# Expert products of a PEER layer: three load buffers per weight, splits one step ahead of their own kind, first product by halves of the tokens

## The chip, the cores and the metric

One core of a Trainium2 chip runs the whole layer in one launch. The metric is the device time of that launch in microseconds (us). The kernel before takes 3207.91 us, the median of three runs (3204.24 to 3208.45). A difference of 0.2% (6.4 us) is about what a measurement of this kernel can tell from no change.

## The reference

The layer is a state-space and convolution mixer, and then a retrieval layer of 16384 one-neuron experts. Only the last part matters here:

```
q = (hf @ wq).reshape(t, 8, 2, 128); s = einsum("thpd,hpkd->thpk", q, sub_keys)
sv, si = top_k(s, 16)                       # 16 of 128 keys on either side
best, flat = top_k(sums of pairs, 16)       # 16 experts of each of 8 heads
experts = i1 * 128 + i2;  gates = softmax(best)
act = gelu(einsum("pd,ped->pe", xb, u_tab[eb]), approximate=False)
out = einsum("pe,ped->pd", gb * act, v_tab[eb])     # 128 experts of each token
```

There are 1024 tokens of 1024 channels, in eight blocks of 128. A gated residual and a final RMSNorm follow. All numbers are float32.

## The kernel before, in words

The kernel is written in one order by hand: each engine executes its instructions in the order in which the program issues them, and a buffer that is still in use makes the engine that wants it wait. Loads of weights are issued on SP's queue, which is also in order: a load whose buffer is not free holds up all loads behind it.

The last stage, the **experts' stage**, is a little over half of the time. Five blocks of tokens (640 tokens, `ND = 5`) take the dense way: the products with *all* experts are formed, 128 experts at a time, and experts that a token did not choose have the gate 0. The other three blocks take the sparse way: they gather the rows of their own experts from DRAM.

*Dense, on TensorE (PE).* A step `In(e)` is the first product of 128 experts: `multiply_u` (L980) multiplies the weights `u`, split in a high and a low part `uh`, `ul` of float32r, with the tokens `hh2`, `hl2`, in 48 matmuls of 320 tokens. Two PSUM tiles `pa` of 320 tokens each take the sums; the pool has three. Then ScalarE (ACT) applies Gelu (`ga`, L1380, one instruction for each half), VectorE (DVE) multiplies with the gates `gm` (L1384), ACT and DVE split the result in `wh` (L1386) and `wl` (L1390). A step `Out` is half of the columns of the second product of 128 experts: 15 matmuls of 512 columns with the weights `v`, split in `vh`, `vl`. Eight `Out` steps sum in PSUM, then DVE adds the sums to the output (L1434). The order of steps is `In` 0 to 7, then again and again 8 `Out`, 1 `In`, 8 `Out`, 7 `In`: 128 `In` and 256 `Out` in all. The first products of e = 0 to 2 are started ahead of the loop.

*Splits.* `hi_lo` (L59, L60): ACT copies to the high part, and the low part is a subtraction, on GpSimd (POOL) for `u`, on DVE for `v`. There are two buffers each of `uh`, `ul`, `vh`, `vl`, and also of the loaded `u`, `v` and `gm`.

*Sparse.* `gathered` (L1266) asks POOL for one row of an expert per token (128 rows of 4 KB, 512 KB, L1275) into one of five buffers `gr`; DVE then forms a dot product (L1297) or adds a multiple (L1309). There are 768 such rows of work. `advance` (L1341) puts them between the steps of the products by fixed shares: 18 units for an `In`, 11 for an `Out`. `choosing` does the choice of experts of the last block beside the first groups. `finish` (L1246) does residual and norm of a sparse block, and borrows two `gr` buffers for it.

What orders the loads and splits is the loop at L1478: at step n the load of step n + 2 is issued, then the split of step n + 1, then the rest of the Gelu step before, then the products:

```
        for x in seq[:2]:
            x.load()
        for n, x in enumerate(seq):
            if n + 2 < len(seq):
                seq[n + 2].load()
            if n + 1 < len(seq):
                seq[n + 1].split()
            ...
            x.mm()
```

Of the kernel before, what the change touches and what calls it, by code (L numbers as in the profile page):

```python
# [8 lines left out]
F32 = mybir.dt.float32  # L9
# [28 lines left out]
ND = 5                   # token blocks whose experts go through dense products; the others gather theirs  # L38
TD = ND * P
TH = TD // 2  # L40
NS = 7                   # token blocks whose experts are chosen before the products
NGB = 5                  # rows of gathered experts on chip
IN_US, OUT_US = 18, 11    # shares of the gather steps beside 128 experts' first product and half of their second
GE = 8                   # blocks of 128 experts between two sums into the output

# The pairs of ranks (i, j) that can be among the top ones: (i + 1)(j + 1) <= 16; those of the upper half have
# (i + 1)(j + 1) <= 8. Pieces are (i0, i1, j0, j1); sums stand in lexicographic order, numbers of experts with the first 20 ahead.
# [15 lines left out]
def mm3(nc, out, a, b, n, start=True, stop=True):  # L63
    """out += sum_k a[k].T @ b[k] in float32 accuracy; a, b give (hi, lo) pairs of a k."""
# [7 lines left out]
def layer_kernel(ctx, tc, A, dbg=None):  # L72
# [8 lines left out]
    # ------------------------------------------------------------------ constants  # L81
# [9 lines left out]
    def rsqrt(dst, src, scale, n):  # L91
        """dst = 1 / sqrt(src * scale + eps) on a small tile, with one Newton step."""
# [15 lines left out]
    row_dram = dram.tile([1, D], F32, name="row_dram")          # gate of the second sublayer  # L108
# [3 lines left out]
    g_dram = dram.tile([ND, 2, P, P, P // 2], F32, name="g_dram")   # gates: [token block, half, second key, first key, token]  # L112
# [32 lines left out]
    # chunks of w_in_t: 0-3 z, 4-7 x, 8-9 B, 10-11 C, 12-15 GLU value, 16-19 GLU gate, 20 dt  # L145
# [14 lines left out]
    def modulate(j):  # L160
        """h1 of the tokens or of the context in [channel, token] layout, split."""
# [9 lines left out]
    # ------------------------------------------------------------------ modulation, norm 1  # L171
    with ExitStack() as st:
# [22 lines left out]
        # sums of squares of the tokens from the transposed tensors  # L195
# [17 lines left out]
        # rows of scale and shift for both conditions, then as columns  # L213
# [52 lines left out]
    # ------------------------------------------------------------------ work beside the matrix products  # L266
    queue, later, spare, call = [], [], [0.0], [0]

    def beside(us):
        """Emits queued instructions that hold VectorE for about this long; a step below zero rests until the next call."""  # L270
# [16 lines left out]
    def ask():  # L287
        """Loads the next two column blocks for modulation()."""
        while asked[0] < 24 and len(ready) < 2:
            j = asked[0]  # L290
            ready[j] = lpr.tile([P, KD, P], F32, name="ld")
            nc.sync.dma_start(ready[j], ada[:, :, 2048 + j * P:2048 + (j + 1) * P])
            asked[0] += 1

    def modulation():
        """The gate of the first sublayer as a row on all partitions, shift and scale of the second as columns."""
# [40 lines left out]
    def key_products():  # L337
        """M = wq @ subkeys.T of every head and side, a half of one at a time."""
# [26 lines left out]
    # ------------------------------------------------------------------ input projection  # L365
    with ExitStack() as st:
# [51 lines left out]
        def layer_norm():  # L418
            """Channel LayerNorm and swish of the convolution group."""
# [26 lines left out]
        def time_steps(pdt):  # L446
            """softplus(v) = max(v, 0) + log1p(e), e = exp(-|v|); log1p by its series where e is small."""
# [25 lines left out]
            # decay to the end of a chunk (times dt), and over a chunk  # L473
# [80 lines left out]
    # ------------------------------------------------------------------ state-space scan, both directions  # L554
# [1012 lines left out]
```

## Time and profile before

| | |
|---|---|
| median of 3 runs | 3207.91 us |
| span of the profiled execution | 3212.8 us |
| PE, DVE, POOL, ACT busy, whole span | 90%, 84%, 62%, 31% |
| experts' stage, from its first product to its last | 1202.3 to 3195.2 us |
| PE, DVE, POOL, ACT busy in that stage | 1864, 1676, 1431, 506 us of 1993 |
| DMA engines busy in that stage | 85%, 296 GB/s |

The profiled execution's own time is not given apart from its span; the span is 0.15% above the median of the runs. A matmul's record is longer than its share of the pipe, so neighbours overlap and PE counts as busy even where it is not at its peak: the distance between starts tells its pace. Waits are put down to the event that came last.

### The profile page before, as it was taken

To read this page: it belongs to the slowest core of one execution; us is meant where nothing else is said; L and a number is where in the kernel's file an instruction comes from. 1 tells how busy PE (TensorE), PEld (TensorE's weight loads), DVE (VectorE), ACT (ScalarE), POOL (GpSimd) and SP (SyncE) were. 2 spreads that over 40 slices of the span, in tenths; PEclk is the share of its full clock that TensorE was granted. 3 is DMA by queue.
4 is the path that set the end of the run, shared out by engine and by line. 5 is a ranking of instruction groups with operands and counts; after the bars stand their busy time and mean duration, and the time that the engine had idled before them with its cause. 6 is when DMAs were issued, how large, how long until landed. Compare 5 with 4: busy or idle time off the path is not lost.

```text
span 3212.8 us, 41810 instructions
## 1 busy us (share of the span) xinstructions
PE 2880.9 (90%) x14905; PEld 2383.1 (74%) x14905; DVE 2693.3 (84%) x4828; ACT 1002.9 (31%) x1584; POOL 2002.0 (62%) x1478
## 2 busy tenths in 40 slices
PE   7999777998888768988999999999999899999996
PEld 4777676754555558877788788888888788888884
DVE  5897888559999997889898887888898888888896
ACT  3224323324555552322222222222222222222222
POOL 0222455316666777777677676776687677777773
PEclk8999998999999879999999999999999999999998
DMA  6111454341212237877888888899889889889883
GB/s 203 59 40 40 127 160 147 99 164 60 85 80 105 105 125 264 314 262 268 298 276 306 303 303 309 315 313 323 302 310 325 303 299 331 308 303 319 303 312 109
DMA packets 334113, 721.09 MB, mean 224 GB/s; under 512 B 24512, under 2 KB 167120, under 8 KB 332624
## 3 DMA queue, kind: packets, MB, share of 16 engines
q0 software_dynamic: 110592, 402.70, 35.5%
q1 hardware_dynamic: 223312, 315.72, 28.6%
q8 instruction: 117, 1.92, 0.2%
q14 instruction: 92, 0.75, 0.1%
HBM read 656.99 MB, written 61.35 MB: 224 GB/s over the span
## 4 chain that ended last, share of the span: by engine, by line
DVE 31%; DMA 19%; PE 18%; issue 16%; POOL 12%; ACT 2%; SPq 0%; POOLq 0%; DVEq 0%; ACTq 0%
POOL gr L1275 7%; DMA gr<-in_peer_v_dram,idx 6%; DMA v<-in_peer_v_dram 5%; DMA gr<-in_peer_u_dram,idx 5%; PE pa L985 4%; PE pa L67 4%; DVE gr L1297 3%; DVE o L1206 2%; POOL ul L60 2%; DVE ob L1198 2%; DVE cfm L407 2%; DVE oh L1076 2%; PE pv L1416 2%; PE pq L946 2%; PE pv L1417 2%
## 5 line engine op out<-in xcount | busy, mean ns | idle before, releaser
L1275 POOL DMA_INDIRECT gr<-in_peer_u_dram,idx x384 | 521.3, 1358 | 216.2 <-DVE gr L1297 130.5
L1275 POOL DMA_INDIRECT gr<-in_peer_v_dram,idx x384 | 504.6, 1314 | 212.4 <-DVE h2T L1309 124.2
L1309 DVE SCALAR_TENSOR_TENSOR h2T<-gr,wv,h2T 128x1024 f32<-128x1024 f32 x381 | 535.5, 1405 | 61.5 <-DMA gr<-in_peer_v_dram,idx 55.1
L1297 DVE SCALAR_TENSOR_TENSOR gr<-gr,h2T 128x1024 f32<-128x1024 f32 x384 | 514.3, 1367 | 73.2 <-DMA gr<-in_peer_u_dram,idx 62.2
L1416 PE MATMUL pv<-vl,wh 128*128 128x512 f32 x1280 | 523.6, 409 | 56.2 <-DVE vl L60 53.9
L1415 PE MATMUL pv<-vh,wl 128*128 128x512 f32 x1280 | 515.5, 403 | 15.2 <-ACT vh L59 15.0
L1417 PE MATMUL pv<-vh,wh 128*128 128x512 f32 x1280 | 512.5, 400 | 0.0
L985 PE MATMUL pa<-hl,uh 128*128 128x320 f32 x2000 | 329.7, 315 | 52.6 <-ACT ga L1380 48.6
L60 POOL TENSOR_TENSOR ul<-u,uh 128x1024 fp32r<-128x1024 f32 x128 | 332.9, 2601 | 66.7 <-ACT uh L59 58.1
L59 ACT ACTIVATE vh<-v 128x512 fp32r<-128x512 f32 x256 | 161.1, 630 | 643.1 <-DMA v<-in_peer_v_dram 522.0
L1416 PEld LDWEIGHTS pv<-vl,wh 128*128 128x128 f32 x1280 | 244.8, 191 | 148.4 <-DVE vl L60 91.9
L985 PEld LDWEIGHTS pa<-hl,uh 128*128 128x128 f32 x2000 | 305.2, 191 | 65.2 <-ACT ga L1380 58.2
L985 PE MATMUL pa<-hh,ul 128*128 128x320 f32 x2000 | 322.2, 315 | 4.5 <-POOL ul L60 4.5
L60 DVE TENSOR_TENSOR vl<-v,vh 128x512 fp32r<-128x512 f32 x256 | 186.4, 728 | 157.0 <-ACT vh L59 152.0
L985 PE MATMUL pa<-hh,uh 128*128 128x320 f32 x2000 | 313.6, 309 | 0.0
L985 PEld LDWEIGHTS pa<-hh,ul 128*128 128x128 f32 x2000 | 307.3, 193 | 5.3 <-POOL ul L60 5.3
L1415 PEld LDWEIGHTS pv<-vh,wl 128*128 128x128 f32 x1280 | 244.7, 191 | 84.0 <-ACT vh L59 26.2
L985 PEld LDWEIGHTS pa<-hh,uh 128*128 128x128 f32 x2000 | 298.4, 188 | 0.0
L1417 PEld LDWEIGHTS pv<-vh,wh 128*128 128x128 f32 x1280 | 244.7, 191 | 54.5
L1200 POOL TENSOR_TENSOR o<-ob,tr 128x512 f32<-128x512 bf16 x160 | 216.1, 1352 | 108.9 <-DVE ob L1198 99.7
L1184 PEld LDWEIGHTS pg<-o,o 128*128 128x128 f32 x1280 | 173.5, 207 | 131.1 <-issue 62.3
L1386 ACT ACTIVATE wh<-ga 128x640 fp32r<-128x640 f32 x128 | 94.8, 740 | 543.5 <-DVE ga L1384 527.3
(351 smaller groups left out, 4661.9 us busy)
## 6 DMA issues: line engine op xcount, KB each, us to landing
u<-in_peer_ut_dram SPq DMA_DIRECT2D x128, 512.0 KB
v<-in_peer_v_dram SPq DMA_DIRECT2D x256, 256.0 KB
g_dram<-stg SPq DMA_DIRECT2D x10, 4096.0 KB
gm<-g_dram SPq DMA_DIRECT2D x64, 640.0 KB
ld<-in_ada_w_dram SPq DMA_DIRECT2D x24, 512.0 KB
w<-in_w_in_t_dram SPq DMA_DIRECT2D x21, 512.0 KB
raw<-in_ada_w_dram SPq DMA_DIRECT2D x8, 1024.0 KB
h2T<-in_wqT_dram SPq DMA_DIRECT2D x16, 512.0 KB
```

The lines of the kernel that those rows point to most:

```text
L59: nc.scalar.activation(hi, src, AF.Copy)
L60: (eng or nc.vector).tensor_tensor(lo, src, hi.bitcast(F32), op=OP.subtract)
L67: nc.tensor.matmul(out, a(k)[i], b(k)[j], start=start and t == 0 and k == 0, stop=stop and t == 2 and k == n - 1)
L985: nc.tensor.matmul(pa[half], x[:, k], y[:, k, half * TH:half * TH + TH], start=t == 0 and k == 0, stop=t == 2 and k == KD - 1)
L1184: nc.tensor.matmul(pg[:, j], o2[:, j], o1[:, j], start=True, stop=True)
L1200: nc.gpsimd.tensor_tensor(o2.rearrange("p t j -> p j t"), ob, tr[:, 1, None, ts].to_broadcast([P, P, 4]), op=OP.mult)
L1275: nc.gpsimd.indirect_dma_start(out=g, out_offset=None, in_=A[t], in_offset=bass.IndirectOffsetOnAxis(ap=idx[:, b, e:e + 1], axis=0))
L1297: nc.vector.scalar_tensor_tensor(g, g, 1.0, h2, op0=OP.mult, op1=OP.mult, accum_out=act[:, e:e + 1])
L1309: nc.vector.scalar_tensor_tensor(ac, g, wv[:, e:e + 1], ac, op0=OP.mult, op1=OP.add)
L1415: nc.tensor.matmul(Out.pv[t], wl[:, sl], self.vh, start=i == 0, stop=False)
L1416: nc.tensor.matmul(Out.pv[t], wh[:, sl], self.vl, start=False, stop=False)
L1417: nc.tensor.matmul(Out.pv[t], wh[:, sl], self.vh, start=False, stop=i == GE - 1)
```

## The change

1. `v` gets three buffers (`NV = 3`). `u` keeps the two of its pool, and every third `u` goes to `spare`, a part of the old token tile `h2T` that held the weights `fw` of the final norm before.
2. `load`, `split` and the new `gate` (the load of `gm`, taken out of `load`) are issued by `begin`, each kind of step in its own order: before a step, splits are issued for the next two steps *of each kind*, and loads for three more. `gm` is issued after the splits and loads of the step.
3. `multiply_u` does all 24 matmuls of the first half of the tokens, then those of the second half.
4. The final norm's weights have no place of their own any more: `finish` loads them into its buffer `rw` after the use of the gate row, and the last dense blocks load them into `spare` near the end. The loads of `finish` and two reloads of the sparse tokens `h2` go from SP's queue to POOL's (11 in all).

```diff
+NU, NV = 3, 3
     def load_u(e):
-        u = e2.tile([P, KD, P], F32, name="u")
+        u = spare if e > 3 and e % 3 == 2 else e2.tile([P, KD, P], F32, name="u")
     def multiply_u(uh, ul, pa):
-        for t, (x, y) in enumerate(((uh, hl2), (ul, hh2), (uh, hh2))):
-            for half in range(2):
+        for half in range(2):
+            for t, (x, y) in enumerate(((uh, hl2), (ul, hh2), (uh, hh2))):
                 for k in range(KD):
         def finish(z, a):
-            nc.sync.dma_start(xt, x1_dram[z * P:(z + 1) * P, :])
+            nc.gpsimd.dma_start(xt, x1_dram[z * P:(z + 1) * P, :])
-            nc.sync.dma_start(rw, row_dram[0].partition_broadcast(P))
+            nc.gpsimd.dma_start(rw, row_dram[0].partition_broadcast(P))
             nc.vector.tensor_tensor(a, a, rw, op=OP.mult)
+            nc.gpsimd.dma_start(rw, A["final_norm_w"].partition_broadcast(P))
         def gathered():
-                    nc.sync.dma_start(h2, h2n_dram[(b + 1) * P:(b + 2) * P, :])
+                    nc.gpsimd.dma_start(h2, h2n_dram[(b + 1) * P:(b + 2) * P, :])
         class Out:
-                self.v = ep2.tile([P, 512], F32, name="v")
+                self.v = ep2.tile([P, 512], F32, name="v", bufs=NV)
-        for x in seq[:2]:
-            x.load()
+        passed = {In: 0, Out: 0}
+        queues = {(kind, what): iter([x for x in seq if isinstance(x, kind)]) for kind, what in
+                  ((In, "load"), (In, "split"), (In, "gate"), (Out, "load"), (Out, "split"))}
+        begun = dict.fromkeys(queues, 0)
+        def begin(kind, what, far):
+            while begun[kind, what] < passed[kind] + far:
+                begun[kind, what] += 1
+                x = next(queues[kind, what], None)
+                if x:
+                    getattr(x, what)()
+        for kind, deep in ((In, NU), (Out, NV)):
+            begin(kind, "load", deep)
         for n, x in enumerate(seq):
-            if n + 2 < len(seq):
-                seq[n + 2].load()
-            if n + 1 < len(seq):
-                seq[n + 1].split()
+            for kind, deep in ((In, NU), (Out, NV)):
+                begin(kind, "split", 2)
+                begin(kind, "load", 2 + deep)
             before = seq[n - 1] if n and isinstance(seq[n - 1], In) else None
             if before:
                 before.weigh()
+            passed[type(x)] += 1
+            begin(In, "gate", 2)
             x.mm()
```

PE, one `In` step in the middle of the stage, before (a row is eight matmuls; `pa_14130` and `pa_14131` are the halves of the tokens; the number behind a name is the buffer's):

```order
L985 MATMUL pa_14130<-hl2_8582,uh_14097 128x320 x8
L985 MATMUL pa_14131<-hl2_8582,uh_14097 128x320 x8
L985 MATMUL pa_14130<-hh2_8581,ul_14098 128x320 x8
L985 MATMUL pa_14131<-hh2_8581,ul_14098 128x320 x8
L985 MATMUL pa_14130<-hh2_8581,uh_14097 128x320 x8
L985 MATMUL pa_14131<-hh2_8581,uh_14097 128x320 x8
```

and now, a like step (line numbers are those of the changed kernel):

```order
L986 MATMUL pa_14432<-hl2_8582,uh_13910 128x320 x8
L986 MATMUL pa_14432<-hh2_8581,ul_13911 128x320 x8
L986 MATMUL pa_14432<-hh2_8581,uh_13910 128x320 x8
L986 MATMUL pa_14433<-hl2_8582,uh_13910 128x320 x8
L986 MATMUL pa_14433<-hh2_8581,ul_13911 128x320 x8
L986 MATMUL pa_14433<-hh2_8581,uh_13910 128x320 x8
```

The second PSUM tile is first needed after 24 matmuls instead of 8, the first one is complete after 24 instead of 40, and the low part `ul` is needed after 8 instead of 16.

ACT, around the single `In` step between two runs of `Out`, before:

```order
L59 ACTIVATE vh_14070<-v_14039 128x512
L59 ACTIVATE uh_14097<-u_14066 128x1024
L59 ACTIVATE vh_14126<-v_14095 128x512
L1380 ACTIVATE ga_14189<-pa_14130 128x320
L1380 ACTIVATE ga_14189<-pa_14131 128x320
L59 ACTIVATE vh_14194<-v_14124 128x512
L1386 ACTIVATE wh_14199<-ga_14189 128x640
```

and now:

```order
L60 ACTIVATE vh_14102<-v_14025 128x512
L60 ACTIVATE vh_14131<-v_14052 128x512
L1384 ACTIVATE ga_14198<-pa_14139 128x320
L1384 ACTIVATE ga_14198<-pa_14140 128x320
L60 ACTIVATE uh_14201<-u_13766 128x1024
L1390 ACTIVATE wh_14208<-ga_14198 128x640
L60 ACTIVATE vh_14238<-v_14079 128x512
```

The split of `u` now stands behind the Gelu and is that of the `In` after the next one; two `vh` of the coming run are made before its first `Out`. Inside a run of `Out` nothing moves: one `vh` a step, before and now.

SP's queue at the start of the experts' stage, before:

```order
L1244 DMA h2T_2111<-in_final_norm_w_dram 128x1024
L1363 DMA gm_9035<-g_dram_83 128x10x128
L1363 DMA gm_9037<-g_dram_83 128x10x128
L971 DMA u_9050<-in_peer_ut_dram 128x1024
L1363 DMA gm_9052<-g_dram_83 128x10x128
```

and now:

```order
L1405 DMA v_9034<-in_peer_v_dram 128x512
L1405 DMA v_9036<-in_peer_v_dram 128x512
L1405 DMA v_9038<-in_peer_v_dram 128x512
L972 DMA u_9040<-in_peer_ut_dram 128x1024
L1405 DMA v_9050<-in_peer_v_dram 128x512
L1405 DMA v_9052<-in_peer_v_dram 128x512
L1367 DMA gm_9054<-g_dram_83 128x10x128
L1367 DMA gm_9056<-g_dram_83 128x10x128
```

The first gates `gm` now stand behind five loads of `v`, two of which wait until the first two `v` are split.

## Rows read from the trace of the kernel before

**Rows 1.** Stretches: us, then PE, PEld, DVE, ACT, POOL busy (x), clock, DMA, GB/s.

```profile
1202.30:1600.00 397.70, 354.68 (x1854) 311.79 (x1854) 334.04 (x683) 106.60 (x172) 290.68 (x229) 0.95 0.81 280
...
2000.00:2200.00 200.00, 194.53 (x1061) 173.10 (x1060) 169.80 (x246) 50.80 (x85) 151.48 (x100) 0.99 0.89 313
...
1202.30:3195.20 1992.90, 1864.40 (x9937) 1635.19 (x9936) 1675.82 (x2166) 506.39 (x828) 1430.99 (x972) 0.98 0.85 296
```

**Rows 2.** Timeline of PE: start, us; two steps' starts, then a pause.

```profile
2219.71 0.40 PE L1415 MATMUL pv<-vh,wl 128*128 128x512 f32 x1
...
2223.20 2.51 PE L985 MATMUL pa<-hl,uh 128*128 128x320 f32 x16
...
2230.24 2.51 PE L985 MATMUL pa<-hl,uh 128*128 128x320 f32 x16
```

**Rows 3.** Timeline of PE: a short pause inside an Out step.

```profile
2204.05 0.50 PE L1415 MATMUL pv<-vh,wl 128*128 128x512 f32 x1
2204.78 0.50 PE L1416 MATMUL pv<-vl,wh 128*128 128x512 f32 x1 [0.23 <-DVE vl L60]
```

**Rows 4.** Waits of PE in the stage: us in total, times, longest.

```profile
PE pv L1416 <- DVE vl L60: 53.9, 66, 5.6
PE pa L985 <- ACT ga L1380: 48.6, 31, 8.8
PE pv L1415 <- ACT vh L59: 15.0, 15, 4.1
PE pa L985 <- POOL ul L60: 4.5, 3, 2.8
```

**Rows 5.** Waits of ACT and of DVE in the stage.

```profile
ACT wh L1386 <- DVE ga L1384: 527.3, 120, 12.2
ACT vh L59 <- DMA v<-in_peer_v_dram: 522.0, 140, 11.5
...
DVE vl L60 <- ACT vh L59: 152.0, 96, 5.4
DVE gr L1297 <- DMA gr<-in_peer_u_dram,idx: 62.2, 46, 4.2
DVE h2T L1309 <- DMA gr<-in_peer_v_dram,idx: 55.1, 47, 4.5
```

**Rows 6.** Timeline of DVE and ACT in a run of Out steps.

```profile
2285.26 0.69 DVE L60 TENSOR_TENSOR vl<-v,vh 128x512 fp32r<-128x512 f32 x1 [1.66 <-ACT vh L59]
...
2291.66 0.64 ACT L59 ACTIVATE vh<-v 128x512 fp32r<-128x512 f32 x1 [2.49 <-DMA v<-in_peer_v_dram]
```

**Rows 7.** Timeline of POOL and DVE in a run of In steps.

```profile
3096.51 2.77 POOL L60 TENSOR_TENSOR ul<-u,uh 128x1024 fp32r<-128x1024 f32 x1
...
3103.96 2.79 POOL L60 TENSOR_TENSOR ul<-u,uh 128x1024 fp32r<-128x1024 f32 x1
...
3096.93 3.03 DVE L1390 TENSOR_TENSOR wl<-ga,wh 128x640 fp32r<-128x640 f32 x1
...
3107.76 0.81 DVE L1390 TENSOR_TENSOR wl<-ga,wh 128x640 fp32r<-128x640 f32 x1
```

**Rows 8.** Timeline of SP's queue, DVE and PE at the start of the stage.

```profile
1210.94 1.06 SPq L1363 DMA_DIRECT2D gm<-g_dram  x2
...
1215.89 0.83 DVE L1384 TENSOR_TENSOR ga<-ga,gm 128x640 f32<-128x640 f32 x1 [5.50 <-DMA gm<-g_dram]
...
1239.40 2.50 PE L985 MATMUL pa<-hl,uh 128*128 128x320 f32 x8 [6.47 <-ACT ga L1380]
```

**Rows 9.** Instructions on `gr` in the stage: ns min/median/max, first and last start.

```profile
L1275 POOL DMA_INDIRECT gr<-in_peer_u_dram,idx x384: 932/1359/1994, 1224.1 to 2811.4; - x192
...
L1275 POOL DMA_INDIRECT gr<-in_peer_v_dram,idx x384: 933/1152/2011, 1556.2 to 3130.4; - x192
```

**Rows 10.** Chain that ended last: two gathers of a row, start and us.

```profile
1301.14 6.59 DMA gr<-in_peer_u_dram,idx
...
1345.07 7.30 DMA gr<-in_peer_u_dram,idx
```

More of the change, by code (lines that the diff above doesn't have):

```diff
@@ L1242, in layer_kernel @@
         acc = h2T[:, :ND]
-        h2, ac, fw = (h2T[:, ND + i] for i in range(3))
-        nc.sync.dma_start(fw, A["final_norm_w"].partition_broadcast(P))
+        h2, ac, spare = (h2T[:, ND + i] for i in range(3))
+        spare_w, spare = spare, spare.rearrange("p (k t) -> p k t", t=P)
         def finish(z, a):
             xt = gp.tile([P, D], F32, name="gr")
-            nc.sync.dma_start(xt, x1_dram[z * P:(z + 1) * P, :])
+            nc.gpsimd.dma_start(xt, x1_dram[z * P:(z + 1) * P, :])
             rw = gp.tile([P, D], F32, name="gr")
-            nc.sync.dma_start(rw, row_dram[0].partition_broadcast(P))
+            nc.gpsimd.dma_start(rw, row_dram[0].partition_broadcast(P))
             for _ in range(5):
@@ L1262, in finish @@
             yield
-            nc.vector.scalar_tensor_tensor(a, a, sf[:, 1:2], fw, op0=OP.mult, op1=OP.mult)
+            nc.vector.scalar_tensor_tensor(a, a, sf[:, 1:2], rw, op0=OP.mult, op1=OP.mult)
             nc.sync.dma_start(A["out"][z * P:(z + 1) * P, :], a)
@@ L1360, in load, with gate @@
                     U[self.e] = load_u(self.e)
+            def gate(self):
                 if self.e % 2 == 0:
@@ L1444, in close @@
                 if t < 2:
-                    nc.gpsimd.tensor_tensor(x, a, fw[:, self.cs], op=OP.mult)
+                    nc.gpsimd.tensor_tensor(x, a, spare_w[:, self.cs], op=OP.mult)
             def post(self):
@@ L1454, in post @@
                         nc.sync.dma_start(Out.rw, row_dram[0].partition_broadcast(P))
+                        nc.sync.dma_start(spare_w, A["final_norm_w"].partition_broadcast(P))
                     X[t] = e2.tile([P, D], F32, name=("u", "uh", "uh", "ul", "ul")[t])
@@ L1502, in layer_kernel @@
             else:
-                nc.vector.scalar_tensor_tensor(acc[:, t], acc[:, t], rs[:, t:t + 1], fw, op0=OP.mult, op1=OP.mult)
+                nc.vector.scalar_tensor_tensor(acc[:, t], acc[:, t], rs[:, t:t + 1], spare_w, op0=OP.mult, op1=OP.mult)
             nc.sync.dma_start(A["out"][t * P:(t + 1) * P, :], acc[:, t])
```

## Prediction

> **What bounds the kernel now.** I read the stretches first, because the change touches only the experts' stage. There the reader is to see three engines near their limit at once: in 1993 us PE is busy 1864, DVE 1676, POOL 1431, and the DMA engines are busy 85% of the time at 296 GB/s [rows 1]. Busy time of PE says little, so I take its pace from the starts. Fifteen matmuls of an `Out` step go from 2219.71 to 2223.20, 3.50 us; an `In` step goes from 2223.20 to 2230.24, 7.04 us [rows 2]. The stage has 127 `In` steps (the first is formed ahead of it) and 256 `Out` steps: 127 x 7.04 + 256 x 3.50 = 1790 us at full pace. It lasts 1993, so it loses 203 us, and this is all that the change can win.
>
> Then I read who PE waits for: 53.9 us in 66 pauses for the low part `vl`, 48.6 in 31 for Gelu `ga` (a PSUM tile that is not yet read), 15.0 in 15 for `vh`, 4.5 in 3 for `ul` [rows 4]. A pause costs more than its idle time, since the weight load in front of the matmul cannot hide: with 0.23 us idle the starts lie 0.73 apart instead of 0.23 [rows 2, 3], so 0.27 us on top. The 115 pauses come to 122 + 31 = 153 us. The mean granted clock of the stage is 0.98 [rows 1], and 2% of 1993 is 40 us; the other 10 are odds and ends of the start.
>
> Last I read why those partners are late. ACT waits 522 us, 140 times, for a load of `v`; it has time for that, but DVE does not: it stands 152 us, 96 times, waiting for `vh`, and 117 us (62.2 + 55.1) for gathered rows [rows 5]. DVE's instructions are in order, so each stall for `vh` delays the rows, the gates' product and the next `vl` behind it.
>
> **The third buffer of `v`.** A buffer of `v` is free when its `vl` is formed and is needed two steps later. In [rows 6] `vl` ends at 2285.95 and the copy of the load that follows into that buffer starts at 2291.66: 5.7 us for the load. With 0.64 for the copy and 0.69 for the subtraction a buffer is bound 7.0 us, and two buffers give a load every 3.5 us, just PE's pace of 3.50 [rows 2, 6]. Every late load is therefore seen. Three buffers give one every 2.3 us, and 3.5 us more lead. Splits inside a run of `Out` stay one step ahead as before, for `vh` and `vl` keep two buffers; but the first two of a run are now made during the `In` steps. What it is worth: the two `v` waits with their restarts are 53.9 + 15.0 + 81 x 0.27 = 91 us [rows 3, 4]. At least the 15.0 for `vh` goes, being a late load or a transition (bound -15), at most all 91. I take the share that DVE's stalls for `vh` have in its stalls for data, 152 of 269 [rows 5]: -51 us.
>
> The Trainium skill (DMA: Bandwidth & Descriptors, section on the anatomy of one DMA on POOL's path) fits a transfer by 2.0 us and its bytes at 436 GB/s, which makes an estimate of 2.6 us for the 256 KB of `v`; by that, two buffers would do, this term would be 0 and the sum -33. The measured 5.7 us decides against it [rows 6].
>
> **The first product by halves.** Before, the second PSUM tile of an `In` step is asked for after 8 matmuls, 1.2 us; it is the tile that Gelu of the step before frees only after PE's last matmul. Now the first half is complete 3.5 us before the step ends, and its tile is asked for 3.5 us into the next step (half of 7.04 [rows 2]). ACT is behind there because it waits for the gates' product on DVE, 527 us in all [rows 5], and DVE and POOL are slow in these steps: a subtraction `ul` on POOL takes 2.77 us, and `wl` on DVE beside it 3.03 instead of 0.81; from one `ul` to the next it is 7.45 us, more than PE's 7.04 [rows 2, 7]. Over a run of seven `In` that lag is 7 x 0.41 = 2.9 us, which 1.2 us of slack does not hold and 3.5 us does; the `Out` steps, with no `ul`, let POOL catch up. The wait is 48.6 + 31 x 0.27 = 57 us, of which 6.5 (the pause at 1239.40, [rows 8]) belongs to the start and stays. Between 0 (it all turns up later as a wait for `vl`) and -57 I take 80% of the remaining 50: -40 us.
>
> **`u` earlier.** The third `u` buffer ends waits that cost PE 4.5 us and a few restarts [rows 4]: -4 us. The number of `ul` in `In` steps is the same, each is one step later.
>
> **The start.** The gates' load now stands behind five loads of `v`. Two of them wait for `vl` of the first two `v`: a load (5.7 at most, [rows 6]), a copy and a subtraction, some 6 us later than 1210.94, and with it the first gates' product at 1215.89 and the first rows [rows 8]. Bounds 0 (PE has products ahead) and +12; I take +6.
>
> **Loads moved to POOL.** Eleven issues of about the 1.3 us of a gather's [rows 9] are 15 us on an engine with 560 us free [rows 1]. What counts is that a reload of `h2`, twice, and the final weights, twice in mid-stage, stand before the next gathers and wait for DVE: one row's period each, (3130 - 1224) / 768 = 2.5 us [rows 9]. Bounds 0 and +15; I take +5. The tail is not longer: POOL has no row left to ask for.
>
> **Next in line.** What is late when `v` is not? The rows. A `gr` buffer comes round every 5 x 2.5 = 12.5 us, 6.6 to 7.3 of it the DMA [rows 9, 10]. When the stage shrinks by 4% its loop shrinks by 0.5 us and DVE's 117 us of waits for rows grow: 0 to +40 on PE, I take +10. The DMA engines move the same bytes: at 1910 us they need 296 x 1993 / 1910 = 309 GB/s, and the stretch from 2000 moved 313 with PE busy 194.5 of 200 [rows 1], so they can. The clock falls after pauses; of its 40 us I give back 10 (bounds 0 and 20).
>
> **Sum:** -51 - 40 - 4 + 6 + 5 + 10 - 10 = -84 us. Against the profiled span of 3212.8 that is 3129; the span is 4.9 us above the median of the runs, so the forecast for the median is 3208 - 84 = **3124 us**. With every term at its better bound (-91 - 57 - 4 - 20) it would be 3036, with every term at its worse one (-15 + 12 + 15 + 40) 3260; they will not all fall on one side, and its own range is 3080 to 3165. Chance 0.66.
>
> **Rivals.** *The rows take the place of `v`.* DVE's 152 us do not vanish but become waits for rows, which are in flight only so deep as five buffers allow. For it: DVE waits for rows 93 times already, and POOL's 7.45 us for an `In` step [rows 5, 7]. Against: from 2000 to 2200 the same loop ran with PE at 97% [rows 1]. Then the `v` term is -15 and the Gelu term halves to -20: with the rest, 3208 - 15 - 20 - 4 + 6 + 5 = 3180 us. Chance 0.15.
>
> *The deeper loads slow the gathers, and it gets slower.* SP's queue now holds up to three `u` and three `v` at once beside three or four rows on POOL's queue, and both use the same engines. Those move 313 GB/s at 89% [rows 1], so about 350 at most; half of that is 175 GB/s, and four rows of 0.52 MB share it for 12 us instead of 6.6 to 7.3 [rows 10]. The loop then takes some 17 us instead of 12.5, and DVE starves. It decides if SP's queue is full for more than a tenth of the stage longer than now: 0.1 x 1993 x 17 / 12.5 - 199 = +72 us at that tenth, which outweighs half of the gains: 3208 + 72 - 42 = 3238 us. Against it: the bytes and so the mean load of SP's queue are the same, and with a load of 5.7 us every 3.5 us there are one to two `v` under way at any time already [rows 6]. Chance 0.11.
>
> The Trainium skill (DMA: Bandwidth & Descriptors, section on queues, rings and completion order) says that each DMA engine takes turns between the queues that have work, packet by packet, which is this rival's mechanism; no run here shows it yet.
>
> *It does not do what it says.* Inside a run of `Out` the copy of the next `v` still waits for the step before last, since `vh` and `vl` have two buffers, so loads that come earlier may only wait longer. Then PE's waits are as before and only start and moved loads remain, with a small gain from the halves: 3208 - 10 + 6 + 5 = 3209 us. Chance 0.08. Against it: 140 of the copies wait for the load [rows 5].
>
> **How the numbers follow.** Faster by over 0.2% (below 3201.5): forecast and first rival, 0.81. Within 0.2%: most of the last, 0.07. Slower: 0.12. The range reaches from the forecast's low end to the first rival with some room, 3080 to 3190; outside it lie the two others (0.19), and the ends of the first two are partly inside a neighbour's.
>
> **What would show it.** In the profile after: ACT's wait for loads of `v` far below 522 us, and in its place waits for PE; DVE's wait for `vh` below 40 of 152 us; PE's wait for `ga` below 15 of 48.6, for `vl` about half of 53.9; the stage near 1910 us; its first gates' product about 6 us later. The forecast is wrong if DVE's waits for rows rise from 117 to over 200 us, or if gathers in the chain take 9 us or more.

## The result and the profile after

The changed kernel takes **3238.03 us** (median of 4 runs, 3229.27 to 3238.87) against 3206.07 for the kernel before (4 runs): ratio **1.009**, 95% interval 1.0073 to 1.0108. It is 32 us slower; forecast were 3124 us. The profiled execution is its fastest run (3229.27 us, span 3227.5), so the two traces lie only 14.7 us apart.

The stretches (us, then PE, PEld, DVE, ACT, POOL busy, clock, DMA, GB/s), to be laid beside [rows 1]:

```profile
1202.30:1600.00 397.70, 347.55 (x1821) 308.92 (x1821) 329.08 (x680) 105.27 (x171) 290.68 (x230) 0.94 0.82 279
2000.00:2200.00 200.00, 192.37 (x1069) 173.56 (x1068) 169.96 (x237) 50.21 (x85) 146.91 (x98) 0.98 0.89 310
1202.30:3209.40 2007.10, 1861.27 (x9942) 1650.46 (x9941) 1692.31 (x2176) 505.00 (x828) 1442.73 (x985) 0.97 0.86 295
```

The stage is 14 us longer, and DVE is busy 16 us more on the same work. That alone is not the loss: in e9 below, which is faster than the kernel before, DVE is busy 1695 us. The waits in the stage (us in total, times, longest), for [rows 4, 5]:

```profile
ACT vh L60 <- PE pv L1421: 667.7, 203, 10.3
...
DVE gr L1299 <- DMA gr<-in_peer_u_dram,idx: 96.3, 66, 4.6
...
DVE h2T L1311 <- DMA gr<-in_peer_v_dram,idx: 81.8, 58, 7.4
DVE vl L61 <- ACT vh L60: 81.4, 76, 4.1
PE pv L1420 <- DVE vl L61: 73.0, 41, 5.6
POOL ul L61 <- ACT uh L60: 69.7, 41, 13.5
...
PE pv L1419 <- ACT vh L60: 50.3, 18, 7.8
...
PE pa L986 <- POOL ul L61: 17.5, 7, 6.1
...
PE pa L986 <- ACT ga L1384: 1.1, 2, 1.0
```

The direct aims were reached: ACT no longer waits 522 us for `v` (it now waits for PE), PE's 48.6 for Gelu are 1.1; DVE's 152 for `vh` are 81, where below 40 was forecast. Yet PE waits more for `vl` (73.0, was 53.9), `vh` (50.3, was 15.0) and `ul` (17.5, was 4.5), and DVE's waits for rows rose from 117 to 178.

Where it went, from the starts of the first matmul of each run of steps on PE's timeline (sums in us; seven `In` at full pace are 7 x 7.04 = 49.3, eight `Out` 28.0; the last of the `Out` stretches behind seven `In` holds 16 steps):

| | before | after | difference |
|---|---|---|---|
| start of the first `Out` run | 1262.24 | 1269.92 | +7.7 |
| first `Out` run | 35.2 | 38.7 | +3.5 |
| 15 runs of seven `In` (median) | 805.1 (52.5) | 756.8 (49.3) | -48.3 |
| 15 stretches of `Out` behind those (median) | 519.9 (30.2) | 573.0 (35.0) | +53.1 |
| 15 single `In` | 109.4 | 105.6 | -3.8 |
| 15 runs of `Out` behind those | 463.2 | 465.1 | +1.9 |

The sum is +14.1, the difference of the starts of the last matmul (3194.97 and 3209.11). The `In` runs go at full pace, and the `Out` runs behind them hand all of it back. How, at the end of one such run (timelines of DVE, POOL, ACT, PE: start, us):

```profile
2283.65 3.87 DVE L1311 SCALAR_TENSOR_TENSOR h2T<-gr,wv,h2T 128x1024 f32<-128x1024 f32 x1 [0.46 <-DMA gr<-in_peer_v_dram,idx]
...
2288.17 0.81 DVE L1388 TENSOR_TENSOR ga<-ga,gm 128x640 f32<-128x640 f32 x1
...
2284.01 2.41 POOL L61 TENSOR_TENSOR ul<-u,uh 128x1024 fp32r<-128x1024 f32 x1
...
2289.01 0.74 ACT L1390 ACTIVATE wh<-ga 128x640 fp32r<-128x640 f32 x1 [6.89 <-DVE ga L1388]
2289.66 1.13 ACT L60 ACTIVATE vh<-v 128x512 fp32r<-128x512 f32 x2
...
2290.32 0.57 PE L1419 MATMUL pv<-vh,wl 128*128 128x512 f32 x1 [3.08 <-ACT vh L60]
```

The `ul` of 2284.01 is the split that the change newly puts into the first `Out` step. DVE's row operation beside it takes 3.87 us instead of some 1.3, the gates' product behind it is late, ACT stands 6.89 us for that with `vh` queued behind `wh`, and PE stands 3.08 us. After the single `In` step the same split does harm in another way (`uh<-h2T` and `ul<-h2T,uh` are the split of a `u` that was loaded into `spare`, a part of `h2T`):

```profile
2322.66 1.05 ACT L60 ACTIVATE uh<-h2T 128x1024 fp32r<-128x1024 f32 x1
...
2323.79 3.28 POOL L61 TENSOR_TENSOR ul<-h2T,uh 128x1024 fp32r<-128x1024 f32 x1 [2.53 <-ACT uh L60]
2327.23 1.76 POOL L1277 DMA_INDIRECT gr<-in_peer_v_dram,idx  x1
...
2334.37 1.28 DVE L1311 SCALAR_TENSOR_TENSOR h2T<-gr,wv,h2T 128x1024 f32<-128x1024 f32 x1 [3.68 <-DMA gr<-in_peer_v_dram,idx]
...
2336.32 0.50 PE L1420 MATMUL pv<-vl,wh 128*128 128x512 f32 x1 [3.00 <-DVE vl L61]
```

`uh` wants the buffer that PE reads until the `In` step ends, POOL stands 2.53 us for it and subtracts 3.28, and the next gather is asked for only at 2327.23. Its row comes 7.1 us later, DVE stands 3.68 us, and PE 3.00 for the `vl` behind that row. These are two places of many; what the split costs in all is left to the experiments.

### The profile page after: what moved, and what is told of

Its sections match the earlier page's. It is cut to its first block, busy times and chain, and to the rows that moved or that the text cites. A ratio compares the mean times of both kernels' runs of the same rounds, so it can differ in the third digit from the quotient of the medians.

```text
span 3227.5 us, 41703 instructions
## 1 busy us (share of the span) xinstructions
PE 2882.4 (89%) x14905; PEld 2402.5 (74%) x14905; DVE 2712.9 (84%) x4828; ACT 1000.5 (31%) x1584; POOL 2010.2 (62%) x1489
## 5 line engine op out<-in xcount | busy, mean ns | idle before, releaser
L1277 POOL DMA_INDIRECT gr<-in_peer_u_dram,idx x384 | 509.9, 1328 | 215.1 <-DVE gr L1299 125.6
L1311 DVE SCALAR_TENSOR_TENSOR h2T<-gr,wv,h2T 128x1024 f32<-128x1024 f32 x381 | 537.3, 1410 | 92.0 <-DMA gr<-in_peer_v_dram,idx 81.8
L1299 DVE SCALAR_TENSOR_TENSOR gr<-gr,h2T 128x1024 f32<-128x1024 f32 x384 | 496.5, 1316 | 103.3 <-DMA gr<-in_peer_u_dram,idx 96.3
L1419 PE MATMUL pv<-vh,wl 128*128 128x512 f32 x1280 | 522.7, 408 | 50.3 <-ACT vh L60 50.3
L1421 PE MATMUL pv<-vh,wh 128*128 128x512 f32 x1280 | 520.8, 407 | 0.0
L986 PE MATMUL pa<-hh,ul 128*128 128x320 f32 x2000 | 338.4, 312 | 17.5 <-POOL ul L61 17.5
L986 PE MATMUL pa<-hh,uh 128*128 128x320 f32 x2000 | 337.4, 311 | 0.0
L986 PEld LDWEIGHTS pa<-hh,uh 128*128 128x128 f32 x2000 | 307.2, 190 | 0.0
L61 POOL TENSOR_TENSOR ul<-u,uh 128x1024 fp32r<-128x1024 f32 x87 | 232.7, 2675 | 50.2 <-ACT uh L60 49.0
L1185 PE MATMUL pg<-o,o 128*128 128x128 f32 x1280 | 190.2, 300 | 76.3 <-DVE o L1207 51.7
L61 DVE TENSOR_TENSOR vl<-v,vh 128x512 fp32r<-128x512 f32 x256 | 185.6, 726 | 82.4 <-ACT vh L60 81.4
```

Of the source, the lines that this page charges most:

```text
L61: (eng or nc.vector).tensor_tensor(lo, src, hi.bitcast(F32), op=OP.subtract)
L986: nc.tensor.matmul(pa[half], x[:, k], y[:, k, half * TH:half * TH + TH], start=t == 0 and k == 0, stop=t == 2 and k == KD - 1)
L1185: nc.tensor.matmul(pg[:, j], o2[:, j], o1[:, j], start=True, stop=True)
L1277: nc.gpsimd.indirect_dma_start(out=g, out_offset=None, in_=A[t], in_offset=bass.IndirectOffsetOnAxis(ap=idx[:, b, e:e + 1], axis=0))
L1299: nc.vector.scalar_tensor_tensor(g, g, 1.0, h2, op0=OP.mult, op1=OP.mult, accum_out=act[:, e:e + 1])
L1311: nc.vector.scalar_tensor_tensor(ac, g, wv[:, e:e + 1], ac, op0=OP.mult, op1=OP.add)
```

## The experiments

All times are medians; ratios are to the kernel before, measured beside it. Theory A: the place of the `u` splits makes the loss. Theory B: the halves, or the deeper loads, do.

### Taking the parts apart

**e1_u_split_late**, the `u` splits in their old place:

```diff
-            for kind, deep in ((In, NU), (Out, NV)):
-                begin(kind, "split", 2)
-                begin(kind, "load", 2 + deep)
+            if n + 1 < len(seq) and isinstance(seq[n + 1], In):
+                begin(In, "split", 2 if isinstance(x, In) else 1)
+            begin(In, "load", begun[In, "split"] - passed[In] + NU)
+            begin(Out, "split", 2)
+            begin(Out, "load", 2 + NV)
```

> The changed kernel with the splits of u placed as before (in the step ahead of the In step that uses them); everything else as changed. Theory of the debt: in a run of seven In steps POOL and DVE need 7.45 us a step and PE 7.04, so PE runs ahead and pays in the next run of Out steps; the change adds to that debt because one ul of 2.8 us moved from the last Out before the run to the first Out after it, and the ul after the single In step makes POOL wait for PE. Undoing this alone gives some 5 us in each of 15 groups less start: about 3210 us, with the Out run after seven In steps back from 33 to 35 us to about 31. Rival (deeper loads slow the gathers): it stays at 3238. Rival (the halves are the cause): it stays near 3235.

Measured 3189.0 us, ratio 0.9939 (0.9915 to 0.9962). One edit turns 32 us slower into 19 us faster. That is more than expected (3210), though the `Out` runs behind seven `In` only come to 32.9 us at the median.

**e2_no_halves**, the changed kernel with `for t` outside `for half` in `multiply_u`:

> The changed kernel with the matmuls of the first product in the order of before (operand by operand, both halves). Theory of the debt: the runs of seven In steps take 51 to 53 us again instead of 49.3, the Out run behind them gets as much shorter, total the same within 8 us: 3230 to 3246. Rival (the halves are the cause, since they let PE run ahead into long pauses that lower the clock): about 3212. Rival (deeper loads): 3238, and the In runs stay slow.

Measured 3239.6 us, 1.0102 (1.0079 to 1.0126): the halves are not the loss, and no gain either.

**e4_halves_alone**, the kernel before with the halves:

> The kernel before with the first product by halves of the tokens; nothing else changed. Theory of the debt: runs of seven In steps fall to 49.3 us, PE's wait for Gelu goes from 48.6 to below 5 us, and the wait for vh and vl takes its place: 3206 within 8 us. Rival (the halves give what I forecast): 3166. Rival (they are the cause of the loss): 3225.

Measured 3207.9 us, 1.0002 (0.9987 to 1.0017). PE's wait for `ga` falls from 48.6 to 2.2, that for `vl` rises from 53.9 to 74.3 and that for `ul` from 4.5 to 23.5. The runs of seven `In` win 35 us (805.1 to 770.0), and the `Out` runs behind them lose 31 (519.9 to 551.2). A moved wait.

**e3_v3_alone**, the kernel before with three `v` buffers, loads of `v` up to three beyond the splits, on the same queue (`load_v`, not shown, does that; `vl[1]` counts the splits):

```diff
+                self.v = ep2.tile([P, 512], F32, name="v", bufs=3)
...
-            if n + 2 < len(seq):
+            if n + 2 < len(seq) and isinstance(seq[n + 2], In):
                 seq[n + 2].load()
             if n + 1 < len(seq):
                 seq[n + 1].split()
+                vl[1] += isinstance(seq[n + 1], Out)
+            if n > 4:
+                load_v()
```

> The kernel before with a third buffer of v and loads of v begun as soon as one is free, three ahead of the splits; nothing else changed. Theory of the debt: the late loads of v go, ACT then waits for PE; the Out runs after a single In step get about 1 us shorter, and the time falls by 5 to 20 us: 3186 to 3201. Rival (deeper loads slow the gathers): 3225 to 3240, with DVE's waits for rows near the 178 us of the changed kernel instead of 117.

Measured 3236.1 us, 1.0091 (1.0069 to 1.0114): as slow as the whole change, though without its `u` splits. The theory failed here, and the time is in the rival's range; DVE's waits for rows are 222.6 us. Its waits:

```profile
ACT uh L59 <- DMA u<-in_peer_ut_dram: 215.6, 47, 10.5
...
POOL ul L60 <- ACT uh L59: 166.1, 41, 9.8
DVE gr L1297 <- DMA gr<-in_peer_u_dram,idx: 114.4, 75, 5.3
DVE h2T L1309 <- DMA gr<-in_peer_v_dram,idx: 108.2, 80, 7.0
```

`u` is late (ACT's wait for it was 57.4 before), POOL stands for `uh` with the gathers queued behind, and rows are late. Whether that was the order of loads, the two `u` buffers or the traffic was open; e6 and e11 tell in part.

**e6_late_no_halves**, e1 operand by operand:

> The changed kernel with the u splits back in their old place (the step before their use) and the first product operand by operand again; against the kernel before it holds the third v buffer, the third u buffer, the loads in each kind's own order and the loads moved to POOL. Theory (the third v buffer lost alone because its loads, ahead in SP's in-order queue, made u late with only two u buffers): with the third u buffer the wait of ACT for u is below 60 us again (215.6 there), and the time is 3185 to 3205. Rival (more loads in flight slow the gathers): VectorE's waits for rows stay above 200 us and the time is above 3225.

Measured 3185.1 us, 0.9937 (0.9912 to 0.9961). The same depth of loads as in the changed kernel, and faster than before: deeper loads by themselves do not slow this kernel.

**e11_two_u** and **e12_two_v**, e6 with `NU, NV = 2, 3` (and no `spare` for `u`), and with `3, 2`:

> The kernel with the late u splits and without halves (3185.1 us), with two buffers for u instead of three. Theory (a third v buffer loses when u has only two, since its loads then stand between u's in SP's in-order queue): ACT's wait for u above 150 us (215.6 where v alone had a third), POOL's wait for uh above 100 us, time 3215 to 3240. Rival (it was the order of issue in that experiment, not the count of u buffers): ACT's wait for u below 80 us, time 3180 to 3195.

> The kernel with the late u splits and without halves (3185.1 us), with two buffers for v instead of three, all else as there. Theory (the third v buffer is what the 20 us against the kernel before come from): 3200 to 3215, ACT's wait for v above 300 us. Rival (the gain is the third u buffer, the order by kinds and the loads moved off SP): 3180 to 3192.

Measured 3186.0 us, 0.9940 (0.9920 to 0.9961), for two `u`; 3213.1 us, 1.0020 (1.0003 to 1.0037), for two `v`. So the third `u` buffer is worth nothing that can be seen, and my reason for e3 (too few `u` buffers) was wrong: with two of them and `u` asked for right behind the split of its own kind, no wait of ACT for `u` is left in the trace. So e3's loss came neither from the count of `u` buffers nor from the third `v` by itself. What is left is the order of the loads on SP's queue; that this made `u` late is argued, since e11 differs from e3 in the place of the `v` splits and in the loads on POOL as well. The third `v` buffer is worth 0.9937 - 1.0020 = -0.8%, 27 us. Its share is read from e12 and then e6:

```profile
DVE vl L61 <- ACT vh L60: 118.9, 96, 4.2
DVE gr L1299 <- DMA gr<-in_peer_u_dram,idx: 77.3, 53, 4.4
...
DVE h2T L1311 <- DMA gr<-in_peer_v_dram,idx: 55.7, 42, 6.7
```

```profile
DVE gr L1299 <- DMA gr<-in_peer_u_dram,idx: 88.3, 66, 4.3
...
DVE h2T L1311 <- DMA gr<-in_peer_v_dram,idx: 69.2, 58, 6.8
DVE vl L61 <- ACT vh L60: 68.7, 74, 3.7
```

DVE's wait for `vh` falls by 50.2, its waits for rows grow by 24.5: 25.7 net, near the measured gain.

### The moved split of u

**e9_u_mid_run**, the changed kernel with that one split at the fifth `Out` step:

```diff
-            for kind, deep in ((In, NU), (Out, NV)):
-                begin(kind, "split", 2)
-                begin(kind, "load", 2 + deep)
+            begin(In, "split", 1 if isinstance(x, Out) and x.i < 4 else 2)
+            begin(In, "load", begun[In, "split"] - passed[In] + NU)
+            begin(Out, "split", 2)
+            begin(Out, "load", 2 + NV)
```

The load of `u` that follows the split moves with it.

> The changed kernel, but the u split that it issues at the first Out step of a run (the one for the In step after next, whose uh buffer PE is still reading) is issued at the fifth Out step; the split that it issues at the last In step of a run stays there. Theory (the price of the moved u splits is this one split: ACT and POOL stand for PE's buffer, with vh, rows and vl queued behind them): 3185 to 3200, PE's wait for vh below 25 us (50.3 in the changed kernel), POOL's wait for uh below 40 us (69.7). Rival (the price is the split beside the last In step, which adds to POOL's arrears): 3225 to 3240.

Measured 3187.3 us, 0.9939 (0.9918 to 0.9961). Its waits:

```profile
DVE gr L1299 <- DMA gr<-in_peer_u_dram,idx: 98.5, 76, 4.3
...
DVE h2T L1311 <- DMA gr<-in_peer_v_dram,idx: 79.0, 58, 6.7
...
POOL ul L61 <- ACT uh L60: 48.6, 34, 13.5
...
DVE vl L61 <- ACT vh L60: 43.1, 37, 4.0
...
PE pv L1419 <- ACT vh L60: 22.5, 12, 5.6
```

Four steps later the split costs nothing: some 50 us (1.0090 against 0.9939) between two kernels that differ in this split and its load alone. The split beside the last `In` step, which stays early here, is not the price, so the rival is out. On PE's timeline the `Out` stretches behind seven `In` fall from 573.0 to 548.6 us and those behind a single `In` from 465.1 to 446.6.

The wait for `vh` came out as expected, on PE (50.3 to 22.5) and on DVE (81.4 to 43.1); POOL's wait for `uh` only fell from 69.7 to 48.6, above the 40 us expected. DVE's waits for rows did not change (178.1 and 177.5 us). So in sum the first of the two ways above, `vh` queued behind a late `wh`, is seen to go; the second, a row that is late because its gather was asked for late, is not, though it too may have been there and been followed by other waits for rows. What the standing for PE's buffer and the `ul` beside DVE's work each cost was not separated.

**e10_u_early_alone**, the kernel before with the `u` splits one step ahead of their own kind (the old loads and splits of `u`, which it leaves out, are not shown):

```diff
...
+            while us[0] < min(NIN, us[2] + 2):
+                U[us[0]] = split_u(U[us[0]])
+                us[0] += 1
+            while us[1] < min(NIN, us[0] + 2, n + 3):
+                U[us[1]] = load_u(us[1])
+                us[1] += 1
+            us[2] += isinstance(x, In)
```

> The kernel before with one change: the u splits one step ahead of their own kind, as in the changed kernel (same buffers, v as before, operand by operand, loads on SP as before, a load of u behind each split). Theory (the moved u splits cost some 50 us by themselves): 3240 to 3260. Rival (they cost only together with the halves or with the v splits that are ahead): 3200 to 3220.

Measured 3259.9 us, 1.0169 (1.0146 to 1.0191): +54 us with none of the other parts. PE's wait for `vl` is 117.1 (53.9 before). A load of `u` then also stands on SP's queue for that split, ahead of loads of `v`; ACT's wait for `v` grew from 522 to 563, so a part may be that.

### Whose arrears the Out runs pay

Arrears are work that an engine still owes when PE moves on to the next run of steps.

**e5_shares** and **e8_late_shares**, the changed kernel and e1 with `IN_US, OUT_US = 16, 12`; **e7_gate_first**, e1 with `begin(In, "gate", 2)` ahead of the first loads:

> The changed kernel, but the gather steps beside an In step are 16 units instead of 18 and beside an Out step 12 instead of 11; the sum over a group stays 320. Theory (the seven In steps ask more of POOL and VectorE than they can do in 7.04 us, the halves let PE run ahead all the same, and the Out steps after them wait for the arrears): fewer rows in the In steps leave less in arrears, the Out runs behind seven In get 1 to 2 us shorter (35.0 us now), 15 times, so 3238 - 15 to 30 = 3208 to 3223. Rival (the arrears come from the ul that the Out steps now start with, whatever the rows): no change, 3233 to 3243.

> The changed kernel with the u splits late (3189.0 us) and shares of 16 and 12 instead of 18 and 11. Theory of arrears: the Out runs behind seven In steps (32.9 us) come down to 31 to 32 us, 15 times, and the time is 3160 to 3175. Rival (the arrears of the In steps are no longer what bounds it; single late loads of v are): within 6 us of 3189.

> The changed kernel with the u splits late (3189.0 us), and the first load of the gates issued ahead of the first loads of u and v instead of behind them. Theory (the start pays 8 us for the gates being late): PE's first Out step in the stage begins 6 to 9 us earlier, and the time is 3180 to 3183. Rival (the start is bound by the splits, or what is won there is waited for later): the first Out is earlier by under 3 us and the time stays 3187 to 3191.

e5: 3222.3 us, 1.0055 (1.0036 to 1.0074). The `Out` behind seven `In` fall from 573.0 to 551.3, as the theory said, but the runs behind a single `In` rise from 465.1 to 484.2; what is left are 11 us by the ratios. e8: 3186.4 us, 0.9933 (0.9908 to 0.9957): 540.5 to 513.1 and 449.6 to 480.6, no gain, as its rival said. With the splits late, spreading the rows otherwise only carries the waits from one run to the other. e7: 3189.5 us, 0.9944 (0.9925 to 0.9962): the first `Out` run begins 5.0 us earlier (1269.36, e1 1274.40), between the two expectations, and the end gains nothing, as the rival said.

**e13_row_half**, **e14_row_half_halves** (e6 and e1 with `[:, :512]` on every operand of a row's operation) and **e15_ul_half**, **e16_ul_half_halves** (e6 and e1 where every second step takes the `ul` of the one before):

> The kernel with the late u splits and without halves (3185.1 us), with VectorE's work on each gathered row cut to half of the columns (the dot products and sums of the other half are left out; gathers as before). It takes some 500 us from VectorE. If VectorE's arrears are what PE's waits come from: below 3130 us, PE's waits for vl and ga below 30 us of 95. If POOL's or the gathers' are: 3165 to 3190.

> The same cut of VectorE's row work in the kernel with the late u splits and with halves (3189.0 us). Theory (the halves only let PE run ahead of arrears, which the Out run then pays): with the arrears smaller the halves are worth more than 0, and this kernel is 5 to 25 us below e13_row_half. Rival (the halves cost something of their own): it is equal to it or slower.

> The kernel with the late u splits and without halves (3185.1 us); every second In step forms no ul and uses the one of the step before (the low parts of half of the u are left out). It takes some 180 us from POOL, and from VectorE the time that it loses beside ul. If POOL's ul are what the seven In steps wait for: In runs at 49.3 us (50.7 there), Out runs behind them below 30 us, 3140 to 3165. If VectorE alone is: 3175 to 3190.

> The same cut of ul in the kernel with the late u splits and with halves (3189.0 us). Theory of arrears of POOL: 3140 to 3165, and the Out runs behind seven In steps (32.9 us) come to some 29 to 30 us. If VectorE alone sets the arrears: 3175 to 3190, and those Out runs stay above 32.

Measured: 3085.9 us (0.9626; 0.9596 to 0.9656) and 3081.1 (0.9609; 0.9580 to 0.9639) with half of the row work, 3139.1 (0.9798; 0.9766 to 0.9831) and 3140.6 (0.9801; 0.9767 to 0.9834) with half of the `ul`. The stretch of 1400 us in the middle, of e6, e13 and e15:

```profile
1600.00:3000.00 1400.00, 1352.33 (x7408) 1207.96 (x7407) 1230.50 (x1386) 363.97 (x591) 1052.15 (x695) 0.99 0.92 318
```

```profile
1600.00:3000.00 1400.00, 1392.57 (x7743) 1256.36 (x7741) 891.65 (x1410) 383.55 (x613) 927.78 (x723) 1.00 0.93 331
```

```profile
1600.00:3000.00 1400.00, 1374.34 (x7578) 1234.02 (x7577) 1168.95 (x1407) 376.30 (x604) 943.73 (x663) 0.99 0.93 326
```

With less to do on DVE, PE runs at its pace (medians of 49.3 and 28.0 us a run), the granted clock is 1.00, and the DMA engines move 331 GB/s. PE's waits for `vl` and `ga` come to 33.2 us, just above the 30 expected. So the DMA engines do not set the pace of the complete kernels; PE waits for arrears of the engines beside it.

The cuts do not tell DVE's arrears from POOL's, as each relieves both engines. POOL asks for the same rows in e13 as in e6, and is still busy 124 us less in the stretch: over the whole stage an issue takes 1.07 us on the mean instead of 1.34 for a row of `u`, and 1.09 instead of 1.33 for a row of `v` (e6, then e13; count | busy us, mean ns | idle time before them and what ended it):

```profile
L1277 POOL DMA_INDIRECT gr<-in_peer_u_dram,idx x384 | 514.8, 1341 | 207.3 <-DVE gr L1299 120.0 <-issue 58.3 <-DVE vl L61 6.6
```

```profile
L1277 POOL DMA_INDIRECT gr<-in_peer_u_dram,idx x384 | 411.8, 1072 | 233.9 <-DVE gr L1299 140.9 <-issue 47.0 <-DMA gr<-in_peer_u_dram,idx 11.4
```

Cutting `ul` brings some 45 us. These times, at the low end of what was expected for arrears of POOL, and the `Out` runs behind seven `In` fit that theory, and not the 3175 to 3190 of VectorE alone. But over the whole stage POOL's busy time falls from 1449.9 us (e6) to 1274.3 (e15), and DVE's falls too, from 1696.9 to 1574.5, 122 us for 62 `ul` fewer. DVE and POOL slow each other, and which of them has to be relieved stays open. The halves are worth 5 us at best once the arrears are gone (e13 to e14), the low end of what was expected, and nothing with half of the `ul`, where the `Out` runs behind seven `In` still differ (medians 28.7 without halves, 29.8 with).

**e17_combined** (e9 operand by operand, gates first) and **e18_combined_shares** (with shares of 17 and 11.5):

> The changed kernel operand by operand, with the first load of the gates ahead of the loads of u and v, and the u split of the first Out step of a run put off to the fifth. Each of the three alone gave what it had to give; if VectorE's work sets the pace (taking half of its row work away brought 99 us), they do not add up: 3175 to 3188. Rival (they remove separate waits): 3160 to 3174.

> The same, with shares of 17 units beside an In step and 11.5 beside an Out step. Theory (VectorE's work as a whole sets the pace; where the rows stand only moves the waits between In and Out runs): within 6 us of e17_combined. Rival (a more even spread lets PE wait less): 8 to 20 us below it.

Measured 3184.5 us, 0.9928 (0.9903 to 0.9953), and 3189.7, 0.9959 (0.9946 to 0.9973). As the theory of DVE's work said, the edits do not add up; a theory of POOL's work would say the same. The best complete versions (e1, e6, e8, e9, e11 and e17) lie some 20 us below the kernel before and cannot be told apart.

## Why the prediction was wrong

A chain of edits from the kernel before to the changed one, the first a bundle and the others single, gives each term (ratios times 3206 us; each is uncertain by some 10 us):

| step | ratio reached | us | forecast |
|---|---|---|---|
| loads by kinds, third `u`, first `v` splits of a run ahead, loads on POOL, gates late (e12) | 1.0020 | +6 | -4 + 6 + 5 |
| third `v` buffer (e6) | 0.9937 | -27 | -51, + 10 for rows |
| `u` splits earlier (e2) | 1.0102 | **+53** | none |
| halves (after) | 1.0090 | -4 | -40 |

**The step that failed first** is the term for the `u` splits: "The number of `ul` in `In` steps is the same, each is one step later." That was the right description and had no price. I did not ask what each later `ul` lands beside: the first `Out` step, where DVE owes PE the gates' product and `wl` of the step before, and POOL the next gathers. Its price is the difference of sign: +53 here, +54 alone (e10), +48 by e1 (ratios), and 48 gone when the split moves four steps on (e9). My own [rows 7] had the hint: `wl` took 3.03 us beside an `ul` instead of 0.81. I used it to explain why `In` steps are slow, not what an `ul` does elsewhere. The price is not that DVE works longer: it is busy 1692 us in the changed kernel and 1695 in e9. It lies in the waits behind the place where the `ul` falls.

**The halves.** "which 1.2 us of slack does not hold and 3.5 us does; the `Out` steps, with no `ul`, let POOL catch up." The first half came true to the tenth (49.3 us a run, wait for `ga` 1.1). The second did not: the lag is not caught up but paid in the `Out` run, as waits for `vl` and `vh`. Nor were the `Out` steps free of `ul`: the change itself puts one into the first `Out` step of each run. The bound "it all turns up later as a wait for `vl`" was the answer, and I gave it a fifth of the term. Measured on three bases, by ratios: +1 (e4), +1 (e6 to e1), -4 (e2 to the changed kernel); none is clear of noise.

**The third `v` buffer** was right in kind and too large. Its bounds, 15 and 91, held the measured 27. "What is late when `v` is not? The rows" was right as well: half of what DVE won at `vh` it lost at rows (50 and 25); both terms together were to be -41. The Trainium skill (DMA: Bandwidth & Descriptors, section on the anatomy of one DMA on POOL's path) gives a fit by which this term would have been 0; e12 and e6 show 27 us. The fit is stated for POOL's path, and the loads of `v` stand on SP's queue beside the gathers, so it is the use of the fit here that fails; no run tests the fit itself.

**Start and moved loads.** The first gates' product came at 1224.32 instead of 1215.89, 8.4 us later (forecast 6); that this costs 6 us at the end is not borne out by e7, where 5 us won there gain nothing.

**Next in line.** The clock gave back nothing: the granted clock of the stage is 0.97 against 0.98, and PE loses 217 us to its full pace there instead of 203.

**The rivals.** "The deeper loads slow the gathers" named 3238 us, the time that came, by luck, for it was not what happened: e6 has the same depth and is faster, and e13 moves 331 GB/s with that depth and with PE at full pace. The first signal that I set for myself (rows above 200 us) did not show either: 178. The second, gathers of 9 us or more in the chain, could tell nothing: before the change the chain already held gathers of up to 10.16 us, not only the 6.6 and 7.3 of [rows 10]. The first rival, rows in the place of `v`, described half of the `v` term.

**What the profile could have told.** PE's waits showed who was late, not whether that engine could be earlier. DVE's idle time gave a hint: it is idle 1993 - 1676 = 317 us, and of these 152 + 117 = 269 are waits for rows and for a `vh` that itself waits mostly for a load [rows 1, 5]. An engine that is nearly always busy or waiting for loads has little time in which to catch up. It is no more than a hint: in e13, where PE sets the pace, DVE waits 368 us for rows and 641 us in all. What the moved split costs shows in DVE's waits, which sum to 304.8 us in the changed kernel and to 258.1 in e9. That these 47 us are near the price of the split is no second proof, since DVE either works or waits and its work is the same.

## What to carry to other kernels

When PE waits for an engine, first add up that engine's busy time and its waits for its own loads. If they nearly fill the stage, more slack on PE's side may only move the wait to the next run, as the halves did here: 48.6 us of waits were taken away, and the time stayed. A trial that takes work from that engine tells more than the sum, if one looks at what else it relieves. A step that is moved gets its price from the place where it lands, so look at three things there: what is queued behind it on its engine, what runs beside it on a shared resource, and whose buffer it asks for there; four `Out` steps (14 us) further on the same split was free. And a deeper buffer is worth what its order on the queue lets it be: the third `v` gave -27 us in one order and stood in a kernel 29 us slower in another.

## What the runs showed of the hardware

A row's operation on DVE in the changed kernel, and the half-size one of e13 (ns min/median/max):

```profile
L1299 DVE SCALAR_TENSOR_TENSOR gr<-gr,h2T x384: 1196/1217/4114, 1241.6 to 2836.0; 128x1024 f32<-128x1024 f32 x192
```

```profile
L1299 DVE SCALAR_TENSOR_TENSOR gr<-gr,h2T x384: 662/691/3204, 1245.0 to 2712.3; 128x512 f32<-128x512 f32 x192
```

The longest is about one `ul` (2.3 to 3.5 us) above the median, at either size: what is lost goes by the length of the other engine's instruction, not by the own one. In the changed kernel 32 of these and the like operations of L1311 took more than twice the median beside a `ul`; each of them ends 1.08 to 1.10 us after that `ul` ends, as if it did its work only then. The Trainium skill (SBUF — State Buffer, section on who interferes with whom) says this of a VectorE instruction with two inputs in SBUF beside a GpSimd instruction that reads SBUF, where the two hold a shared port in turn and the other stands until it is free; these rows agree. In 9 of the 32 the record of DVE's operation begins up to 0.61 us before that of the `ul`, and it stands all the same. What had not been expected is the size in sum: 122 us of DVE's busy time for 62 `ul`, 2.0 us each, on one of the two engines whose arrears PE waits for.
